# A hybrid decoder layer on one core: half of the per-layer projection moved into the local attention, and the last gate begun inside the MLP

## The chip, the cores and the metric

The kernel runs on one core of one Trainium2 chip. The metric is the device time of one execution in microseconds (us). Before the change the median of three runs is 864.67 us, the lowest 863.82 and the highest 864.80.

A core has five engines that matter here. TensorE (PE in the profile) multiplies matrices and turns (transposes) tiles, and its weight load is listed as PEld. VectorE (DVE) and ScalarE (ACT) do elementwise work. GpSimd (POOL) and SyncE (SP) mostly issue transfers (DMAs). [...]

## What is computed

The layer works on 512 tokens of width 1024. Its reference, cut to what matters here:

```python
h = rmsnorm(x, norm_mix_g)
proj = h @ w_in                                   # split into 9 parts
y_a = sigmoid(o_ml) * h_ml                        # mLSTM branch
y_b = swa_with_sinks(q_sw, k_sw, v_sw, sinks)     # local attention, 16 query heads, window 128
merged = sigmoid(g_a) * (y_a @ w_branch_a) + sigmoid(g_b) * (y_b @ w_branch_b)
x = x + merged @ w_out
x = x + square(relu(rmsnorm(x, norm_mlp_g) @ w_up)) @ w_down
gate = sigmoid(rmsnorm(x, norm_ple_g) @ w_ple_gate)
x = x + gate * (p @ w_ple_proj)                   # p: 512 x 256, w_ple_proj: 256 x 1024
out = rmsnorm(x, final_norm_g)
```

The per-layer projection is `p @ w_ple_proj`. It depends on inputs alone, so it can be done at any time before the gate is multiplied with it. In the text x2 is the value of x after the MLP, scaled by `norm_ple_g` and turned so that its 1024 features lie along the partitions: eight columns of 128 features, numbered 0 to 7. The gate product `x2 @ w_ple_gate` sums over these eight columns, two at a time, so that it has four chunks (numbers 0 to 3: columns 0 and 1, 2 and 3, 4 and 5, 6 and 7).

## The kernel before, in words

**Numbers.** Every float32 operand of a product is split into a high part and a low part (`split`, line 199): ACT casts the high part, DVE subtracts it from the value for the low part. A product is then three matmuls, high x high, high x low, low x high (`pairs`, line 233). A weight is loaded by SP into one of four raw buffers ("wr"), and its two parts go to one of four pairs of buffers ("wh", "wl") in `load_w` (line 221).

**Order.** The program is straight-line code for a list scheduler, which orders each engine's work ahead of time: what the code names first goes first as soon as its inputs are taken to be ready, and what comes later fills in. `tc.issue_after(i)` queues a block's instructions behind instruction `i` on `i`'s engine. `tc.keep_in_program_order` pins an instruction behind the one before it. For the MLP the class `Plan` (line 36) replaces this: its tasks have an engine, a cost and predecessors, the TensorE tasks stand in a written order, the others get due times from it, and `plan.run` emits all of them pinned (line 91).

**Stages.** First come the norm of x and the first half of the per-layer projection (512 of 1024 columns, `early_products`), whose result is parked in device memory in the tensor `ped` (lines 306 and 525). Then follow the input projections, the local attention (lines 865 to 968), the mLSTM, the branch products, the output projection, and the MLP in four quarters (`up_set`, `down`). The tail is what comes after `plan.run()` (line 1759).

**Local attention.** There are 16 units of scores and softmax (`swa_probs`, line 869), each with eight matmuls into a two-bank tile "psa", an eviction by DVE or ACT, and a softmax on both. Between the units the loop at line 961 pops a list `fill` of ten projections (line 957), one at each `u` that is not a multiple of three. A projection is 24 matmuls of 512 columns into one bank "psg"; there are two such banks (`ps_g`, line 157). `qk_proj` (line 849) empties its bank with one ACT instruction (line 852) and three DVE instructions (line 854).

**End of the MLP.** `down(3)` multiplies in seven products by sums and differences of blocks. The last of them (`w4`, line 1734) is two halves of 12 matmuls each into the two "psg" banks. Its result is added into `xk`, the running x, by `acc(Y, 0, 0)` (line 1735, DVE line 1690): tokens 0 to 255, feature columns 0 to 511. The columns 512 to 1023 are complete earlier, after line 1733.

**Tail.** `ple_rows` and `load_w(w_pp[1])` bring p and the second half of `w_ple_proj` and split them. `two_columns_of` (line 1208) turns two columns of x2 with eight transposes (line 1213) and splits them with `gple`, which is an ACT eviction (line 205) and a DVE one (line 206) for each column. Between them stand the four products `ple(m)` of six matmuls, which make the second half of the per-layer projection and are copied by ACT into `pe[m]` (line 1781). Then come the gate's first 512 output columns in four chunks of 24 matmuls (lines 1853 to 1861) into four banks `pv`, and then its second 512 columns with sigmoid, merge and final norm.

## Time and profile before

The profiled execution took 864.57 us by the clock of the runs; the span from its first to its last instruction is 862.7 us, so that 1.9 us lie around the span.

| what | value |
| --- | --- |
| median of the runs shown | 864.67 us |
| profiled execution | 864.57 us, span 862.7 us |
| granted TensorE clock | 0.998 |
| local attention, from first scores to the first branch product | about 228 to 322 us of the span |
| last half product of the MLP ends, tail begins | 801.4 us |
| second half of the gate begins | 832.4 us |
| last matmul ends | 855.3 us |

In the profile's groups each row names line, engine and operation, the output and input tiles, the shape, how often it ran, the busy time and the mean of one in ns, and the idle time before it. Matmuls overlap in the pipeline: a row gives each 0.39 us, but their starts are 0.227 us apart, and it is the distance of the starts that fills PE's time. In the timeline a row gives the start, the length, and in brackets the idle time before it with what ended it.

### The profile page before, as it was taken

What the parts mean: (1) busy time and instruction counts of PE and PEld (TensorE: products, weight loads), DVE (VectorE), ACT (ScalarE), POOL (GpSimd) and SP (SyncE); (2) the same over time, 40 slices, a digit from 0 to 9 for tenths busy, and PEclk for the clock granted to TensorE, in tenths of its full rate; (3) what the DMA queues carried; (4) which work ended last, traced back from release to release, by engine and by line L of the source; (5) the groups of instructions that cost most, each with busy time, mean ns of one, the idle gap of its engine ahead of it and who ended that gap; (6) DMA issues with size and microseconds to landing.
All of it is one profiled execution on the core that took longest, in us unless ns stands there. A gap on an engine that the chain in (4) does not pass through costs nothing.

```text
span 862.7 us, 12945 instructions
## 1 busy us (share of the span) xinstructions
PE 851.6 (99%) x4926; PEld 741.1 (86%) x4926; DVE 724.1 (84%) x1059; ACT 530.4 (61%) x913; POOL 61.2 (7%) x93
## 2 busy tenths in 40 slices
PE   9999999999999999999999999999999999999996
PEld 7888789999878777888888888899889989988886
DVE  7898879777788888867897799879988997899656
ACT  6776657555587667864343586458638744774743
POOL 3121111000000000000020000000000000010000
PEclk9999999999999999999999999999999999999999
DMA  8677235444411246565324381744365364634402
GB/s 289 204 179 295 89 144 189 155 147 146 148 49 50 98 147 226 202 252 200 122 39 133 98 234 38 221 129 137 75 193 147 104 174 133 172 104 131 138 1 97
DMA packets 37967, 125.70 MB, mean 146 GB/s; under 512 B 5261, under 2 KB 5261, under 8 KB 37906
## 3 DMA queue, kind: packets, MB, share of 16 engines
q1 hardware_dynamic: 28578, 95.77, 32.6%
q0 software_dynamic: 9184, 28.85, 13.9%
q8 instruction: 38, 0.62, 0.3%
q10 hardware_dynamic: 144, 0.26, 0.1%
q14 instruction: 23, 0.19, 0.1%
HBM read 106.51 MB, written 11.54 MB: 137 GB/s over the span
## 4 chain that ended last, share of the span: by engine, by line
PE 86%; issue 5%; DVE 4%; ACT 2%; DMA 2%; SPq 0%; POOL 0%; POOLq 0%; DVEq 0%; ACTq 0%
PE psp L1382 27%; PE psg L241 24%; PE psa L241 11%; PE psg L1382 9%; PE psp L241 6%; PE pst L241 4%; ACT lm L900 1%; DMA wr<-in_w_vsif 1%; PE psp L1213 1%; PE pst L945 1%; PE psa L875 1%; PE psa L876 1%; PE psa L911 1%; DVE wl L203 0%; DMA wh<-in_w_b 0%
## 5 line engine op out<-in xcount | busy, mean ns | idle before, releaser
L202 ACT CAST wh<-wr 128x1024 fp32r<-128x1024 f32 x90 | 94.8, 1054 | 81.1 <-PE psg L241 20.9
L203 DVE TENSOR_TENSOR wl<-wr,wh 128x1024 fp32r<-128x1024 f32 x90 | 109.5, 1220 | 35.7 <-ACT wh L202 35.3
L1382 PE MATMUL psp<-x,wh 128*128 128x256 f32 x672 | 121.3, 283 | 0.0
L1382 PE MATMUL psp<-wh,uf 128*128 128x512 f32 x336 | 106.1, 390 | 0.1
L1382 PEld LDWEIGHTS psp<-x,wh 128*128 128x128 f32 x672 | 105.0, 192 | 0.3
L1367 ACT CAST wh<-wr 128x1024 fp32r<-128x1024 f32 x59 | 60.5, 1049 | 59.7 <-DVE wr L1707 26.4
L1382 PE MATMUL psp<-x,wl 128*128 128x256 f32 x336 | 95.1, 283 | 0.0
L1370 DVE TENSOR_TENSOR wl<-wr,wh 128x1024 fp32r<-128x1024 f32 x59 | 71.2, 1219 | 10.3 <-ACT wh L1367 8.0
L1382 PEld LDWEIGHTS psp<-wh,uf 128*128 128x128 f32 x336 | 63.1, 188 | 14.3 <-issue 1.3
L1367 ACT CAST wh<-wd 128x1024 fp32r<-128x1024 f32 x45 | 47.2, 1049 | 33.0 <-PE psp L1382 27.8
L1382 PE MATMUL psp<-wl,uf 128*128 128x512 f32 x168 | 65.5, 390 | 0.0
L1382 PEld LDWEIGHTS psp<-x,wl 128*128 128x128 f32 x336 | 64.5, 192 | 0.0
L241 PE MATMUL psg<-h,wh 128*128 128x512 f32 x192 | 60.9, 395 | 0.7 <-DVE acc L854 0.7
L1370 DVE TENSOR_TENSOR wl<-wd,wh 128x1024 fp32r<-128x1024 f32 x45 | 54.7, 1218 | 3.1 <-ACT wh L1367 3.1
L241 PEld LDWEIGHTS psg<-h,wh 128*128 128x128 f32 x192 | 35.1, 188 | 7.5 <-DVE acc L854 0.9
L1400 DVE TENSOR_TENSOR uf<-F,uf 128x512 fp32r<-128x512 f32 (+3 forms) x36 | 35.0, 983 | 6.4 <-ACT uf L1399 6.4
L241 PE MATMUL psg<-yb,wh 128*128 128x512 f32 x128 | 40.0, 392 | 0.0
L241 PE MATMUL psg<-h,wl 128*128 128x512 f32 x96 | 37.7, 393 | 0.0
L1382 PEld LDWEIGHTS psp<-wl,uf 128*128 128x128 f32 x168 | 31.5, 188 | 6.7 <-DVE wl L1370 0.3
L1382 PE MATMUL psg<-wh,uf 128*128 128x512 f32 x112 | 36.5, 389 | 0.0
L1399 ACT CAST uf<-F 128x512 fp32r<-128x512 f32 (+3 forms) x36 | 30.7, 857 | 7.6 <-DVE F L1417 7.1
L241 PE MATMUL psg<-ya,wh 128*128 128x512 f32 x112 | 34.9, 391 | 0.0
(409 smaller groups left out, 2221.6 us busy)
## 6 DMA issues: line engine op xcount, KB each, us to landing
wr<-in_w_down SPq DMA_DIRECT2D x16, 512.0 KB, 4.6
wd<-in_w_down SPq DMA_DIRECT2D x16, 512.0 KB, 4.4
wr<-in_w_upb SPq DMA_DIRECT2D x12, 512.0 KB, 4.2
wd<-in_w_upb SPq DMA_DIRECT2D x12, 512.0 KB, 4.5
gd<-gr POOLq DMA_DIRECT2D x8, 512.0 KB, 2.9
wr<-in_w_qkml SPq DMA_DIRECT2D x8, 512.0 KB, 3.4
wr<-in_w_b SPq DMA_DIRECT2D x8, 512.0 KB, 3.4
wh<-in_w_b POOLq DMA_DIRECT2D x8, 512.0 KB, 4.6
```

What stands on the lines that cost most here:

```text
L202: A.copy(dst[0], src)
L203: last_low[0] = V.tensor_sub(dst[1], src, r32(dst[0]))
L241: last_mm[0] = T.matmul(ps, l, r, start=first and i == 0, stop=last and i == len(ops) - 1, skip_group_check=parts)
L875: T.matmul(o, q[:, n * P : (n + 1) * P], kk[kp][ab][:, k0 : k0 + 256], start=True, stop=False)
L876: T.matmul(o, q[:, n * P : (n + 1) * P], kl[kp][ab][:, k0 : k0 + 256], start=False, stop=True)
L900: A.activation(lm3[:, g, :], lm3[:, g, :], AF.Exp, bias=nmx[:, g : g + 1], scale=0.125, accum_out=sm[:, g : g + 1])
L911: T.transpose(pt[:, c : c + P], pT[:, c : c + P], ident)
L1367: return [A.copy(parts[0], slots[user])]
L1370: return [V.tensor_sub(parts[1], slots[user], r32(parts[0]))]
L1382: yield T.matmul(ps, l, r, start=first and j == 0, stop=last and j == len(ops) - 1, skip_group_check=True)
L1399: h = sca(n / 512 * 0.48 + 0.05, lambda: A.copy(dst()[0], src()), deps)
L1400: return vec(n / 512 * 0.54 + 0.06, lambda: V.tensor_sub(dst()[1], src(), r32(dst()[0])), [h])
```

## The change

Three things are done together. The second half of the per-layer projection becomes `ple_rest`, an eleventh entry of `fill`, and is stored to `ped`, which gets 1024 columns; the loop pops one entry more, at `u` = 0. The columns 4 to 7 of x2 are turned by `right_columns`, tasks of the plan that stand between the two halves of the last product. Chunk 2 of the gate becomes tasks of the plan too (`first_gates`), behind the last product. After the plan the columns 0 and 1 are turned, then chunk 3 follows, the columns 2 and 3, and the chunks 0 and 1. Each of these later chunks has its weight's cast queued on ACT behind the eviction of the columns turned last.

```diff
-    ped = dp.tile([P, NT, 512], F32, name="ped")
+    ped = dp.tile([P, NT, D], F32, name="ped")
...
-            nc.gpsimd.dma_start(out=ped[:, m, :], in_=early_pe[m])
+            nc.gpsimd.dma_start(out=ped[:, m, :512], in_=early_pe[m])
...
+    def ple_rest():
+
+        rows, w = load_w(p, 1024, 2), load_w(w_pp[1], 1024, 2)
+        for m in range(NT):
+            ps = ps_g()
+            mm_tok(ps, w, [[q[:, k, :] for q in rows] for k in range(2)], m)
+            t = act_f("pl")
+            A.copy(t, ps)
+            nc.gpsimd.dma_start(out=ped[:, m, 512:], in_=t)
...
-    fill = [lambda: qk_proj(0)] + [lambda i=i: q_proj(i) for i in range(5, 8)]
+    fill = [lambda: qk_proj(0), ple_rest] + [lambda i=i: q_proj(i) for i in range(5, 8)]
...
-        if u % 3:
+        if u % 3 or u < 3:
             fill.pop(0)()
...
-        acc(Z, 1, 1, u3)
-        w4, u4 = both(Y, A22, "b21", t4, False, True, y2)
+        z2 = acc(Z, 1, 1, u3)
+        w4[0], _ = half(Y, A22, "b21", 0, t4[0], False, True, y2)
+        if q == 3:
+            right_columns(sum(y2 + z2, []))
+        w4[1], u4 = half(Y, A22, "b21", 1, t4[1], False, True, y2)
         acc(Y, 0, 0, u4)
...
+    def turn(bank, k, m):
+        return T.transpose(bank[:, m * P : (m + 1) * P], xk[m][:, k * P : (k + 1) * P], ident)
+
+    def right_columns(deps):
...
+        spent = role[:2]
+        bank = lambda k: spent[k // 2 - 2][:, k % 2, :]
+        free = done_with[id(spent[0])] + done_with[id(spent[1])]
+        for k in range(4, KT):
+            v = plan.add("PE", 0.45, lambda k=k: (turn(bank(k), k, m) for m in range(NT)), deps + free + plan.last("PE"))
...
+            v = plan.add("ACT", 0.55, high, [v])
+            x2_ready[k] = vec(0.7, low, [v])
...
+    def first_gates():
+
+        X, Y, Z = role
+        w = form(("pg", 2), 2, [load("wr", w_pg[2], ("pg", 2))])
+        for m in range(NT):
+
+            def emit(got, m=m):
+                ops = []
+                for k in range(2):
+                    ops += pairs([q[:, m * P : (m + 1) * P] for q in x2[4 + k]], [q[:, k, :] for q in got])
+                return [(pv[m], ops, True, False)]
+
+            on_pe(w, 1.37, emit, [x2_ready[4], x2_ready[5]] + done_with[id(Z)])
...
+    pv = [role[0][:, 0, :], role[0][:, 1, :], role[2][:, 0, :], role[2][:, 1, :]]
+    first_gates()
     plan.run()
...
-    pT = ple_rows()
-
-    wp1 = load_w(w_pp[1], 2 * 512, 2)
...
+    def gate_chunk(c):
+        with tc.issue_after(turned_2[-1]) if turned_2 else ExitStack():
+            w = load_w(w_pg[c], 2 * 512, 2)
+        for m in range(NT):
+            ops = []
+            for k in range(2):
+                ops += pairs([q[:, m * P : (m + 1) * P] for q in x2[2 * c + k]], [q[:, k, :] for q in w])
+            chain(pv[m], ops, False, c == 1, True)
+
+    turned_2 = []
+
+    def left_columns(k, banks):
+        for c in range(2):
+            for m in range(NT):
+                turn(banks[c], k + c, m)
+        for c in range(2):
+            evicted = split(x2[k + c], banks[c], gple[:, k + c : k + c + 1])
+        turned_2.append(evicted.ins)
+        return evicted
+
+    left_columns(0, [role[1][:, 0, :], role[1][:, 1, :]])
+    gate_chunk(3)
+    evicted = left_columns(2, [ps_g(), ps_g()])
+    gate_chunk(0)
     nc.sync.dma_start(out=gfin, in_=g_fin.broadcast_to([P, D]))
     for m in range(NT):
-        nc.gpsimd.dma_start(out=pe[m][:, :512], in_=ped[:, m, :])
...
+        nc.gpsimd.dma_start(out=pe[m], in_=ped[:, m, :])
...
+    gate_chunk(1)
```

The old loops over `two_columns_of`, `ple` and the four chunks of `pv` go away. The second half of the gate and all that follows it are unchanged.

## Prediction

> **What bounds the kernel now.** I read the page first, then the chain of waits, then PE's waits, then the two places that the change touches, in windows and in the timeline.

> ```profile
> span 862.7 us, 12945 instructions
> PE 851.6 (99%) x4926; PEld 741.1 (86%) x4926; DVE 724.1 (84%) x1059; ACT 530.4 (61%) x913; POOL 61.2 (7%) x93
> PE 86%; issue 5%; DVE 4%; ACT 2%; DMA 2%; SPq 0%; POOL 0%; POOLq 0%; DVEq 0%; ACTq 0%
> ```

> PE is busy in 851.6 of 862.7 us, and the chain that ended last is PE for 86% of the span. The change takes no matmul and no transpose away; it moves them. So it can only gain what PE loses today, and it loses what PE will newly wait. PE's waits by name are few:

> ```profile
> PE psg L343 <- DVE zero L281: 1.1, 1, 1.1
> PE pst L945 <- DVE pT L918: 0.7, 1, 0.7
> PE psg L241 <- DVE acc L854: 0.7, 1, 0.7
> PE psa L875 <- DVE lm L889: 0.2, 1, 0.2
> PE psa L911 <- DVE nmx L893: 0.2, 1, 0.2
> ```

> The 1.1 us are the start and stay. Four waits lie in the local attention, 1.8 us in all, and the 0.7 of line 945 comes at its very end, after the last filler. What the new filler can cover at the beginning is 0.7 + 0.2 + 0.2 = 1.1 us. The windows say the same: outside 228 to 260 PE is full, and in the tail too.

> ```profile
> 228.00:246.00 18.00, 17.41 (x94) 14.26 (x93) 14.94 (x36) 14.34 (x44) 0.00 (x0) 1.00 0.17 60
> 246.00:260.00 14.00, 13.48 (x69) 9.49 (x70) 13.71 (x32) 10.54 (x37) 0.00 (x0) 1.00 0.27 79
> 260.00:275.00 15.00, 15.00 (x86) 12.84 (x86) 12.12 (x34) 11.07 (x40) 0.00 (x0) 1.00 0.20 67
> 801.40:810.80 9.40, 9.40 (x58) 7.93 (x57) 6.46 (x9) 7.19 (x12) 0.00 (x0) 1.00 0.16 63
> ```

> The columns are length, then busy time of PE, PEld, DVE, ACT and POOL, then PE's clock. PE lacks 0.59 and 0.52 us in the first two and nothing in the others. So the attention has about one microsecond to fill, and the change puts five into it.

> **Part 1, the projection in the attention.** It is 24 matmuls of 512 columns. The chain shows what such a group takes, and what sixteen transposes and the four gate chunks take:

> ```profile
> 265.58 5.45 PE psg L241 x24
> 484.35 1.75 PE psp L1213 x16
> 810.83 21.76 PE psp L241 x96
> ```

> The attention gets 5.44 us of PE work (21.76 / 4). On the other engines come two casts and four bank copies on ACT and two subtractions on DVE, by these rows of the tail, where their like stands today:

> ```profile
> 796.16 1.05 ACT L202 CAST wh<-wr 128x1024 fp32r<-128x1024 f32 x1 [1.66 <-PE psp L1382]
> 804.89 0.58 ACT L1781 COPY pe<-psg 128x512 f32<-128x512 f32 x1
> 808.67 1.22 DVE L203 TENSOR_TENSOR wl<-wr,wh 128x1024 fp32r<-128x1024 f32 x1 [0.51 <-ACT wh L202]
> 222.46 36.61 SPq L218 DMA_DIRECT2D wr<-in_w_qkml  x7
> ```

> ACT gets 2 x 1.05 + 4 x 0.58 = 4.4 us and DVE 2.4 us. From 228 to 260 ACT is free for 32 - 24.9 = 7.1 us and DVE for 32 - 28.65 = 3.35 us, and the stretch grows by five, so throughput suffices. On SP two loads now stand ahead of the later projections' weights; SP ran ahead there (seven loads spread over 36.6 us, waiting for raw buffers), so I take that at nothing; if a weight came late, PE would wait for its load. POOL gets four stores of 256 KB, and it was idle in these windows.

> What the filler needs is not engines but banks. A projection keeps one of the two "psg" banks until it is evicted, and this is how long that takes today:

> ```profile
> 236.49 0.39 PE L241 MATMUL psg<-h,wl 128*128 128x512 f32 x1
> 237.67 0.63 PE L241 MATMUL psg<-h,wh 128*128 128x512 f32 x2
> 242.91 0.39 PE L241 MATMUL psg<-h,wl 128*128 128x512 f32 x1
> 246.37 0.73 PE L241 MATMUL psg<-h,wh 128*128 128x512 f32 x2 [0.66 <-DVE acc L854]
> 236.98 0.40 ACT L900 ACTIVATE lm<-lm,nmx 128x128 f32<-128x128 f32 x1
> 241.90 0.67 ACT L852 ACTIVATE acc<-psg,cw 128x512 f32<-128x512 f32 x1
> ```

> The first projection's last matmul is at 236.49. ACT goes through the exponentials of three units from 236.98 to 241.90 and only then touches the bank, and DVE gives it back at 246.3, where PE has waited 0.66 us. In between PE lives on one projection of 5.4 us in the other bank (237.67 to 243.14). After the change the next filler is not one product of 24 matmuls in a bank but four of 6 (1.36 us each), and each wants its own eviction by ACT. If ACT keeps to its exponentials, the second bank is full at 237.67 + 1.36 = 239.0 and comes back at 241.90 + 0.58 = 242.5: 3.4 us in which PE has little else. They would replace the waits of 0.66 and 0.24 us seen there now, a net loss of 2.5 us. Against this, the first projection now precedes unit 2's scores in the code, and its eviction the softmax of unit 2, so the first bank should return earlier. The extra cost beyond 5.44 therefore lies between -1.1 (every wait filled) and +2.5. I take 0, nearer to the row of waits than to the row of the exponentials, because of that earlier place.

> **Part 2, the tail without the projection.** These rows bound it today:

> ```profile
> 801.41 0.38 PE L1213 MATMUL psp<-ident,xk 128*128 128x128 f32 x2
> 810.66 0.39 PE L241 MATMUL psp<-wh,x 128*128 128x512 f32 x1
> 832.42 0.39 PE L241 MATMUL psg<-wh,x 128*128 128x512 f32 x1
> ```

> From the first transpose to the first matmul of the gate's second half are 832.42 - 801.41 = 31.01 us. What must still be done there (or, for the right columns, inside the last product) is 32 transposes, 2 x 1.75 = 3.50, and the four chunks, 21.76: together 25.26. So 5.75 us go: 5.44 of the projection and 0.3 of switching. That holds if PE does not wait.

> **Part 3, the right columns.** They need the additions after the last but one product:

> ```profile
> 796.17 1.41 DVE L1690 SCALAR_TENSOR_TENSOR xk<-psp,r,xk 128x512 f32<-128x512 f32 x2 [0.41 <-PE psp L1382]
> 796.13 5.44 PE psg L1382 x24
> 801.61 0.75 DVE L1690 SCALAR_TENSOR_TENSOR xk<-psg,r,xk 128x512 f32<-128x512 f32 x1 [0.61 <-PE psg L1382]
> ```

> Those are done at 797.6; the first half of the last product ends at 796.13 + 2.72 = 798.85, so the transposes start without a wait. The second half (2.72 us) covers the eviction of columns 4 and 5, and chunk 2 finds them ready. These transposes are pinned, and behind them queue the rest of the last product and chunk 2: were the additions late by more than 1.2 us, all of that would shift. The last addition (801.61 to 802.36 today) is covered by chunk 2's 5.44 us.

> **Part 4, the new wait.** When chunk 2 ends (call it T), PE turns columns 0 and 1. Chunk 3 needs only the columns 6 and 7, which are ready, but its weight's cast is queued on ACT behind the eviction of column 1. Today the first chunk's weight is cast at 796.16, fourteen microseconds before its use at 810.66; that cover is gone. The new chain, by these rows and those above:

> ```profile
> 803.53 1.45 ACT L205 ACTIVATE x<-psp,gple 128x512 fp32r<-128x512 f32 x2 [6.31 <-PE psp L1213]
> 807.54 1.10 ACT L202 CAST wh<-wr 128x1024 fp32r<-128x1024 f32 x1
> L1213 PE MATMUL psp<-ident,xk 128*128 128x128 f32 x64 | 8.0, 273 | 0.0
> ```

> Column 0 is turned at T + 0.44 + 0.27 = T + 0.71. Two evictions, 1.45, end at T + 2.16. The cast, 1.10, ends at about T + 3.2 (ACT's rows overlap by 0.1), and chunk 3's first matmul can go. The second needs the low part, 1.22 on DVE: T + 4.4. PE's eight transposes end at T + 0.87; the transposes of columns 2 and 3 can fill to T + 1.74. Then PE stands for 1.46 us, does the first matmul of each of the four banks (0.91 us), and stands 0.3 us more: 1.8 us. The ends are 0 (the transposes slip in during chunk 2, so that the evictions are over at T) and 3.5 (nothing fills T + 0.87 to T + 4.4). I take 1.8, because today's list puts transposes of a later pair ahead wherever PE is free. The chunks 0 and 1 have 5.44 us of cover each.

> Of the transfers, the load of `pe` is twice as large and the final gain's load moves back in SP's queue:

> ```profile
> L1776 POOL DMA_DIRECT2D pe<-ped x4: 898/900/909, 767.7 to 769.4; - x4
> L1810 DVE TENSOR_TENSOR prod<-sgp,pe x11: 415/426/692, 830.6 to 855.9; 128x256 f32<-128x256 f32 x6, 128x512 f32<-128x512 f32 x5
> DMA to landing us min/median/max: 5.9/6.7/8.3
> ```

> The first use is at 830.6 and the loads are issued at 768; even at 16.6 us, twice the longest landing, they are hidden by some 45 us.

> **The sum.** Against the execution's own 864.57 us: -5.75 + 1.8 (tail) + 5.44 + 0 (attention) = +1.5, so 866.1 us. That execution is 0.1 us below the median of 864.67. About 0.2% (1.7 us: 862.9 to 866.4) is what a measurement of this kernel can tell from no change, so the forecast is no measurable change, on its slow side.

> **The rivals.**
> *The banks stall the attention (slower).* One mechanism: two banks, four small products and an ACT that is in the exponentials. It decides where ACT's copy of the first small product is put behind the third unit's exponentials. For it: ACT ran without a break from 236.98 to 241.90, and the bank of line 852 waited for it. Against it: the earlier place of the first projection. Price: +2.5, 868.6 us.
> *The tail does not wait.* If the left transposes find gaps in chunk 2, the 1.8 us vanish: 864.57 - 5.75 + 5.44 = 864.3, no change. For it: the list does move work forward. Against: chunk 2 is pinned, always ready, and named earlier.
> *Everything fills (faster).* The same, and the attention's 1.1 us are covered, and the 0.7 at its end too because the softmax has got ahead: 864.3 - 1.8 = 862.5. Against it: three conditions at once.
> *The clock falls.* The window behind the last matmul shows PE's clock after idleness:

> ```profile
> 855.00:857.00 2.00, 0.32 (x3) 0.11 (x1) 1.26 (x4) 1.63 (x2) 0.00 (x0) 1.00 0.68 262
> 858.00:859.00 1.00, 0.00 (x0) 0.00 (x0) 0.49 (x1) 0.46 (x1) 0.00 (x0) 1.00 0.00 0
> 859.00:860.00 1.00, 0.00 (x0) 0.00 (x0) 0.00 (x0) 0.00 (x0) 0.00 (x0) 0.53 0.65 252
> ```

> PE ends at 855.3, and the clock halves at about 859.1, 3.7 us later. Chunk 2's end is followed by 1.7 us of transposes and 1.5 us of waiting, 3.2 us without an ordinary matmul. If transposes counted as idleness and the pause grew a little, the next 3.7 us would run at half speed: +1.85, 867.9 us. [...] The row of 801.40 to 810.80 has 32 transposes with the clock at 1.00, but matmuls lie between them, so no run here shows it yet.

> **How the numbers follow.** Forecast 0.40 (its own range 865.3 to 866.9; 0.30 within 0.2%, 0.10 slower), banks 0.27 (slower), no wait in the tail 0.18 (0.15 within, 0.03 faster), everything fills 0.10 (faster), clock 0.05 (slower). Together faster 0.13, same 0.45, slower 0.42. The range reaches from 863.0, near the case in which everything fills, to 868.9, just over the bank case; outside are the rest of the fast case and the 3.5 us end of the tail's wait on top of the bank case.

> **What would show it.** In the profile after: the tail's stretch from the end of the last product to the first 256-column matmuls shorter by about 4 us; an idle time of PE of 1 to 2 us before chunk 3, ended by ACT line 202 or DVE line 203; the attention longer by about 5.4 us; its waits on DVE line 854 gone, or in their place a wait on the ACT copy of `ple_rest`. I am wrong if chunk 3 starts without a wait, if PE stands over 2 us between 236 and 248, or if any part before 228 or between 360 and 795 changes its length.

## The result, and the profile after

The changed kernel takes 874.92 us (median of five runs, 873.29 to 875.90), the kernel before 864.80 (863.82 to 864.98): a ratio of 1.0117, 95% interval 1.0102 to 1.0132. It is slower by 10 us, and the forecast of 866.1 us with its range to 868.9 was wrong. The profiled execution took 875.62 us. The head of its page:

```profile
span 873.8 us, 12968 instructions
PE 856.6 (98%) x4926; PEld 743.4 (85%) x4926; DVE 724.6 (83%) x1059; ACT 530.6 (61%) x913; POOL 63.5 (7%) x97
```

The span grew by 11.1 us, and PE's busy time by 5.0 although PE has the same 4926 instructions. So one part of the loss is standing, and another is that the same matmuls take longer. PE's waits (in total, how often, the longest; the 1.1 us of the start left out):

```profile
PE psg L241 <- ACT pl L872: 4.0, 1, 4.0
PE psp L241 <- ACT wh L202: 2.6, 1, 2.6
...
PE psa L1035 <- DVE hd L1059: 0.9, 1, 0.9
PE psg L241 <- DVE acc L854: 0.4, 2, 0.3
```

The first two are new. One lies in the attention, one in the tail.

**The attention.** ACT's timeline (start, length, instruction), then PE's:

```profile
235.46 1.05 ACT L202 CAST wh<-wr 128x1024 fp32r<-128x1024 f32 x1 [3.98 <-PE psg L241]
236.53 1.28 ACT L907 ACT_TABLE_LOAD   x1
237.83 0.20 ACT L907 ACTIVATE es<-ds 128x4 f32<-128x4 f32 x1
...
241.23 0.69 ACT L852 ACTIVATE acc<-psg,cw 128x512 f32<-128x512 f32 x1
...
242.29 0.60 ACT L872 COPY pl<-psg 128x512 f32<-128x512 f32 x1
```

```profile
238.66 0.28 PE L886 MATMUL psa<-kl,qs 128*128 128x256 f32 x1
242.94 0.50 PE L241 MATMUL psg<-wh,wh 128*128 128x512 f32 x1 [4.00 <-ACT pl L872]
...
243.92 0.63 PE L241 MATMUL psg<-wh,wh 128*128 128x512 f32 x1
244.35 0.63 PE L241 MATMUL psg<-wl,wh 128*128 128x512 f32 x1
```

PE finishes the projection's first product at 237.8 and a unit's scores at 238.9. Then both "psg" banks (128 x 512 float32 each, by these rows) are full, one with the convolution's product, one with this one. ACT is in the exponentials of two units from 237.83 to 241.21, does two other evictions, and copies the bank out from 242.29 to 242.89; PE's next product into it starts at 242.94. The product that waits is the second of the projection (its four start at 236.44, 242.94, 245.58 and 248.40); the expectations below call it the third. Afterwards the starts of the matmuls are 0.43 us apart, not 0.227: PE runs at half its clock (0.50 in the windows below).

**The tail.** First PE, then ACT:

```profile
809.68 1.91 PE L1759 MATMUL psp<-ident,xk 128*128 128x128 f32 x16
811.34 0.48 PE L1392 MATMUL psg<-wh,uf 128*128 128x512 f32 x1
...
819.62 1.03 PE L1759 MATMUL psp<-ident,xk 128*128 128x128 f32 x8
820.49 1.04 PE L1759 MATMUL psg<-ident,xk 128*128 128x128 f32 x8
824.10 0.80 PE L241 MATMUL psp<-wh,x 128*128 128x512 f32 x1 [2.57 <-ACT wh L202]
```

```profile
820.69 0.69 ACT L205 ACTIVATE x<-psp,gple 128x512 fp32r<-128x512 f32 x1 [7.51 <-PE psp L1759]
821.28 1.26 ACT L205 ACTIVATE x<-psg,gple 128x512 fp32r<-128x512 f32 x2
822.42 0.70 ACT L205 ACTIVATE x<-psp,gple 128x512 fp32r<-128x512 f32 x1
822.99 2.95 ACT L202 CAST wh<-wr 128x1024 fp32r<-128x1024 f32 x3
```

The right columns are turned and chunk 2 runs without a wait. Then ACT evicts column 0, the columns 2 and 3 (x2, out of "psg"), and only then column 1, and chunk 3's cast is queued behind that. PE stands for 2.57 us, and about 0.5 more for the low part (its wait is listed as 0.5 us, ended by DVE line 203, in the tail alone; here it lies within the half clock).

**The clock.** These windows are the cells of a grid of 3.41 us (how the grid was found stands at the end). The fields with a multiplication sign are busy time and instructions of PE, PEld, DVE, ACT and POOL; the number behind them is PE's clock:

```profile
240.10:243.51 3.41, 0.57 (x2) 0.48 (x3) 2.81 (x6) 3.25 (x10) 0.33 (x1) 1.00 0.07 28
243.51:246.92 3.41, 3.23 (x8) 2.13 (x7) 3.41 (x8) 1.29 (x8) 0.21 (x1) 0.50 0.19 77
...
820.37:823.78 3.41, 1.16 (x11) 0.92 (x9) 2.37 (x4) 3.09 (x5) 0.00 (x0) 1.00 0.01 2
823.78:827.19 3.41, 3.06 (x6) 2.01 (x7) 3.41 (x5) 3.41 (x6) 0.00 (x0) 0.50 0.25 66
827.19:830.61 3.42, 3.42 (x9) 2.67 (x8) 2.86 (x5) 3.35 (x8) 0.00 (x0) 0.50 0.89 291
```

A cell in which PE hardly worked (busy 0.57 and 1.16 us) is followed by one, or two, at half clock: 3.4 us in the attention, 6.8 us in the tail.

**The balance.** Before, the last product starts at 795.97 and the gate's second half at 832.42; after, at 806.95 and 843.82. So the tail takes 36.87 us instead of 36.45, and the other 11.0 us arise ahead of it. There: 5.4 of moved work, 4.0 of standing for the bank, 1.7 of half clock, 0.7 more ahead of line 1035, less 1.2 of old waits (the attention's 1.8 us of them shrank to 0.6): 10.6, which leaves about 0.4 without a name. In the tail: -5.75 + 2.6 + 0.5 + about 3 of half clock = +0.4.

The theory to be tested (called W): two stands, each behind a FIFO on ACT, and a clock that falls because PE stands.

### The profile page after: what moved, and what is told of

The parts are those of the page before. It is cut to its first block, busy times and chain, and to the rows that moved or that the text cites. A ratio compares the mean times of both kernels' runs of the same rounds, so it can differ in the third digit from the quotient of the medians.

```text
span 873.8 us, 12968 instructions
## 1 busy us (share of the span) xinstructions
PE 856.6 (98%) x4926; PEld 743.4 (85%) x4926; DVE 724.6 (83%) x1059; ACT 530.6 (61%) x913; POOL 63.5 (7%) x97
## 4 chain that ended last, share of the span: by engine, by line
PE 86%; issue 5%; DVE 5%; ACT 2%; DMA 0%; POOL 0%; POOLq 0%; DVEq 0%; ACTq 0%
PE psp L1392 28%; PE psg L241 24%; PE psa L241 11%; PE psg L1392 9%; PE psp L241 5%; PE pst L241 4%; PE pst L955 1%; ACT lm L910 1%; ACT wh L202 1%; DVE wl L203 1%; PE psa L885 0%; DMA wh<-in_w_b 0%; DVE acc L854 0%; PE psa L921 0%; PE psa L886 0%
## 5 line engine op out<-in xcount | busy, mean ns | idle before, releaser
L202 ACT CAST wh<-wr 128x1024 fp32r<-128x1024 f32 x90 | 94.2, 1052 | 86.9 <-PE psg L241 27.6
L203 DVE TENSOR_TENSOR wl<-wr,wh 128x1024 fp32r<-128x1024 f32 x90 | 109.5, 1221 | 38.5 <-ACT wh L202 38.0
L1380 DVE TENSOR_TENSOR wl<-wr,wh 128x1024 fp32r<-128x1024 f32 x60 | 72.4, 1219 | 11.5 <-ACT wh L1377 9.3
L241 PE MATMUL psg<-h,wh 128*128 128x512 f32 x192 | 60.6, 394 | 0.3 <-DVE acc L854 0.3
L241 PEld LDWEIGHTS psg<-h,wh 128*128 128x128 f32 x192 | 35.4, 188 | 8.2 <-issue 0.8
L241 PE MATMUL psg<-yb,wh 128*128 128x512 f32 x128 | 40.2, 393 | 0.0
L241 PE MATMUL psg<-h,wl 128*128 128x512 f32 x96 | 37.9, 395 | 0.0
L241 PE MATMUL psg<-ya,wh 128*128 128x512 f32 x112 | 34.9, 391 | 0.0
```

Of the source, the lines that this page charges most:

```text
L202: A.copy(dst[0], src)
L203: last_low[0] = V.tensor_sub(dst[1], src, r32(dst[0]))
L241: last_mm[0] = T.matmul(ps, l, r, start=first and i == 0, stop=last and i == len(ops) - 1, skip_group_check=parts)
L1380: return [V.tensor_sub(parts[1], slots[user], r32(parts[0]))]
```

## The experiments

Each kernel was timed beside the kernel before on the same chip; the kernel before had medians of 864.27 (beside each part alone, chunk 3's cast first, and the copies on DVE), 864.04 (beside the three casts, the spare banks, the later place and the added matmuls) and 864.45 (beside the last four). Beside the changed kernel it had 864.80, so a gain over the changed kernel, given below as a difference of medians, is up to 0.8 us smaller when each kernel is set against the kernel before beside it.

### One part at a time

The attention part alone: the kernel before, plus (the function `ple_rest` and the wider `ped` left out here)

```diff
-    fill = [lambda: qk_proj(0)] + [lambda i=i: q_proj(i) for i in range(5, 8)]
+    fill = [lambda: qk_proj(0), ple_rest] + [lambda i=i: q_proj(i) for i in range(5, 8)]
...
-        if u % 3:
+        if u % 3 or u < 3:
...
```

> The kernel before, with the new projection function in the list of fillers and the tail untouched, so that the second half of the per-layer projection is computed twice (the tail uses its own). It holds the attention part of the change and nothing else. Theory W (waits and clock): the added 24 matmuls cost 5.4 us, the third product stands 4.0 us on its bank because the copy that empties it is queued on ACT behind two units' exponentials, and the clock is halved for some 3 us behind that, 1.4 us: with the small waits that shift, about +11 us, so near 876. The forecast's own bounds: +4.3 to +7.9, so 869 to 873. Rival S (the loss belongs to the sum of both parts, for instance a memory layout that the new tail brings): +5.4, so 870, and no stand of over 1 us ahead of the projection's third product.

Measured: 876.62 us, ratio 1.0146 (1.0129 to 1.0164). PE's waits:

```profile
PE psg L241 <- ACT pl L872: 4.0, 1, 4.0
PE psa L1035 <- DVE hd L1059: 2.2, 1, 2.2
```

The tail alone, which is the changed kernel without `ple_rest`:

```diff
-    fill = [lambda: qk_proj(0), ple_rest] + [lambda i=i: q_proj(i) for i in range(5, 8)]
+    fill = [lambda: qk_proj(0)] + [lambda i=i: q_proj(i) for i in range(5, 8)]
...
+            nc.gpsimd.dma_start(out=ped[:, m, 512:], in_=early_pe[m])
...
```

> The changed kernel without the new projection function: the second half of the per-layer projection is left out, and the first half's values stand in its place. It holds the tail part of the change and nothing else. Theory W: from the last product's start to the second half of the gate the tail takes what it took before or 0.4 us more, since the 5.75 us that go are eaten by a wait of 2.6 us ahead of the third chunk and 3 us of half clock behind it: 865, no difference that can be measured. The forecast: 5.75 us go and 1.8 come back, so 861. Rival S: the wait ahead of the third chunk comes from what the attention part moved, and is gone here: 859.

Measured: 863.40 us, ratio 0.9988 (0.9979 to 0.9997). The wait is there without the attention part:

```profile
PE psp L241 <- ACT wh L202: 2.6, 1, 2.6
```

The whole loss is in the attention part, 12.4 us; the tail part gains 0.9 us of its 5.75. Their sum, 11.5, is within 1.5 us of the change's 10.1, so rival S falls. The stand of 4.0 us is the same to the tenth.

### The tail's wait

```diff
-    left_columns(0, [role[1][:, 0, :], role[1][:, 1, :]])
-    gate_chunk(3)
+    w3 = load_w(w_pg[3], 2 * 512, 2)
+    left_columns(0, [role[1][:, 0, :], role[1][:, 1, :]])
+    gate_chunk(3, w3)
...
```

> The changed kernel, with the load and cast of the weights of the tail's chunk 3 issued ahead of the left columns, so that the cast isn't queued on ACT behind any of their evictions. Theory W: the wait of 2.6 us goes, the clock then has no reason to fall (3.2 us), and 0.3 us of waiting for the low parts goes: -6, so 869. Rival K (chunk 3 waits for something that comes just after the cast, or the cast only moves the wait to the next chunk): -1 or less, so 874. Rival C (the clock falls because of the 16 transposes and not because of the wait): -2.6, so 872, and the granted clock still falls to 0.5 in the tail.

Measured: 875.27 us (872.64 to 878.50), ratio 1.0131 (1.0108 to 1.0154): no gain at the median. ACT's timeline and PE's wait show that the wait has moved:

```profile
826.85 1.26 ACT L205 ACTIVATE x<-psg,gple 128x512 fp32r<-128x512 f32 x2 [3.72 <-PE psg L1759]
828.00 1.99 ACT L202 CAST wh<-wr 128x1024 fp32r<-128x1024 f32 x2
```

```profile
PE psp L241 <- ACT wh L202: 1.9, 1, 1.9
```

Chunk 3 went without a wait, and chunk 0 stood instead, for its own cast behind the evictions of columns 2 and 3. That is rival K; theory W, which took the wait for gone, was too quick. The profiled execution is one of the shortest. It has no half clock in the tail, which takes 33.71 us in it, 3.2 less than in the changed kernel. The two longest had the lowest mean clocks (0.990 and 0.991, the others 0.993 to 0.995); what else they lost was not recorded. The next kernel takes all three casts out of the queue:

```diff
+    w3, w0, w1 = [load_w(w_pg[c], 2 * 512, 2) for c in (3, 0, 1)]
     left_columns(0, [role[1][:, 0, :], role[1][:, 1, :]])
-    gate_chunk(3)
+    gate_chunk(3, w3)
...
```

> The changed kernel, with the loads and casts of the weights of all three later chunks of the tail (3, 0 and 1) issued ahead of the left columns. ACT stood idle for 5 to 6 us between the right columns' evictions and the left ones', and three casts take 3.2 us. Where chunk 3's cast alone went first, PE stood 1.9 us for chunk 0's cast instead, behind the evictions of columns 2 and 3. Theory W (each chunk's cast is queued on ACT behind evictions; stands of PE cost their own length and, where they leave a grid cell of 3.41 us with less than about 1.4 us of PE work, 1.7 or 3.4 us more in half clock): no stand over 0.5 us from the last product to the second half of the gate, and no half clock there: -2.9 of waits and -1.7 to -3.4 of clock, 869 to 870. Rival K (the left columns or the low parts come last, and the wait moves once more, to chunk 0's columns or DVE's low parts): 872 to 875, with a stand ended by DVE L206 or L203.

Measured: 869.52 us, ratio 1.0064 (1.0051 to 1.0076), 5.4 us under the changed kernel. One window from the last product to the second half of the gate:

```profile
806.00:843.50 37.50, 37.50 (x184) 31.42 (x183) 23.26 (x34) 23.04 (x37) 0.00 (x0) 1.00 0.21 71
```

PE has no gap and the full clock. (The list now also puts the transposes of the columns 2 and 3 behind the start of chunk 3.) From the last product's start to the gate's second half it takes 30.79 us; 36.45 - 5.75 = 30.70 had been worked out for a tail without waits.

### The bank in the attention

```diff
-            A.copy(t, ps)
+            V.tensor_copy(t, ps)
```

> The changed kernel, with the four copies that empty the projection's banks put on DVE instead of ACT. DVE stood idle from 237.8 to 239.6 us in the profile after, just when the first copy was wanted. Theory W: the stand of 4.0 us ahead of the third product falls under 1 us and the clock stays up behind it; the copies take 4 x 0.7 us on DVE and cost up to 1 us where they delay the convolution: -4.5, so 870 (869 to 872). Rival L (load: the added work of ACT and DVE is what slows the attention, whichever engine has it, as the units behind it wait for their probabilities): no gain, 874 to 876, with the wait moved to the score or turn instructions.

Measured: 874.84 us, ratio 1.0124 (1.0110 to 1.0138). The stand shrinks only from 4.0 to 2.4 us. From the first full scores (near 228) to the first branch product the profiled execution takes 105.1 us, against 105.9 in the changed kernel and 94.9 before, and the median doesn't move. DVE's timeline:

```profile
239.13 0.16 DVE L911 TENSOR_TENSOR sm<-sm,es 128x4 f32<-128x4 f32 x1 [1.84 <-ACT lm L910]
...
239.54 0.69 DVE L914 TENSOR_TENSOR lm<-lm,rc 128x512 f32<-128x512 f32 x1
240.15 0.68 DVE L872 COPY pl<-psg 128x512 f32<-128x512 f32 x1
```

DVE was idle for 1.84 us, but with line 911 at the head of its queue, which waited for ACT's exponentials, and the copy stood behind it and began at 240.15. The idle time was no help to an instruction that was queued behind a waiting one. A cell at half clock was left as well (the clock is 0.83 from 237 to 243 and 0.76 from 243 to 246). This run alone would have spoken for rival L. Other banks tell the two apart:

```diff
-            ps = ps_g()
+            ps = ps_g() if m == 2 else ps_t()
```

> The changed kernel, with the projection's products 0, 1 and 3 written to the pair of one-bank tiles that the attention's sums use only later, and product 2 to the pair shared with the weight projections. The copies stay on ACT where they were. Theory W: three products run without a stand, the fourth waits for the first's copy (near 243) for about 1.2 us; no half clock: -2.8 of waits and -1.7 to -3.4 of clock, 870 to 871. Rival L (ACT and DVE are what the attention waits for, and PE only waits somewhere else if it doesn't wait here): the stand moves to the next weight projection or to a turn (ended by DVE L854 or L894) and the time stays at 874 to 875.

Measured: 869.12 us, ratio 1.0061 (1.0048 to 1.0074), 5.8 us under the changed kernel:

```profile
PE psp L241 <- ACT wh L202: 2.6, 1, 2.6
PE psa L1035 <- DVE hd L1059: 1.6, 1, 1.6
PE pst L241 <- ACT pl L872: 1.3, 1, 1.3
```

ACT and DVE have as many instructions as before (913 and 1059), and on ACT the same exponentials and evictions still stand ahead of the first copy; what follows it the list has put in another order. The 4.0 us are 1.3, no half clock follows in the attention, and its stretch takes 100.8 us instead of 105.9. So it was the banks, and rival L falls. The same function three places later in the list:

```diff
-    fill = [lambda: qk_proj(0), ple_rest] + [lambda i=i: q_proj(i) for i in range(5, 8)]
+    fill = [lambda: qk_proj(0)] + [lambda i=i: q_proj(i) for i in range(5, 8)] + [ple_rest]
```

> The changed kernel, with the projection put fifth in the list of fillers (behind the query projections 5 to 7) and not second. Its banks, its copies on ACT and its length are the same. Theory W (its stand comes from the one burst of ACT work at the pipeline's start: a table load and the exponentials of two units, back to back, while all units' scores that the banks allow are done): no stand over 1 us and no half clock in the attention; -4.0 and -1.7 to -3.4: 868 to 870. Rival Q (four evictions in 5.4 us on two banks are too many anywhere in this stage, where ACT always has a unit's exponentials queued): stands of 2 to 4 us show up at the new place, 872 to 876.

Measured: 872.79 us, ratio 1.0098 (1.0084 to 1.0112), 2.1 us better, about a third of what theory W said, and within rival Q's range. The projection itself no longer waits, and none of Q's stands of 2 to 4 us appears. But the scores and turns wait, in pieces of up to 0.9 us:

```profile
PE psa L885 <- DVE lm L899: 1.4, 2, 0.7
...
PE psa L921 <- DVE lm L894: 0.9, 1, 0.9
PE psg L241 <- DVE acc L854: 0.7, 1, 0.7
```

Two of them lie within one cell of the grid (266.57 to 269.98, 1.80 us in the busy column), and a cell at half clock (0.50) follows. Neither theory had this, and why the pieces arise there was not tested.

### The clock

Twelve matmuls more in each of the two stands (the code also names chunk 3 behind the transposes of the columns 2 and 3, where PE did it anyway):

```diff
             mm_tok(ps, w, [[q[:, k, :] for q in rows] for k in range(2)], m)
+            if m == 0:
+                spare_bank = ps_t()
+                for _ in range(12):
+                    T.matmul(spare_bank, rows[0][:, 0, :P], w[0][:, 0, :], start=True, stop=True)
...
+    for i in range(12):
+        T.matmul(pv[i % NT], zero, x2[4][0], start=False, stop=False, skip_group_check=True)
...
```

> The changed kernel with added matmuls in its two stands, and nothing else in another place: twelve products of the projection's operands into a bank that nobody reads, behind the projection's first product, and twelve products with a matrix of zeros, accumulated into the gate's banks, behind the left columns' transposes. The results stay as they are, and so do the waits: the third product still has to wait for ACT's copy (until about 243) and chunk 3 for its cast. 12 x 0.227 = 2.7 us of the stands of 4.0 and 2.6 us are filled. Theory W: the clock is what falls when PE stands, so no half clock in the attention or in the tail; the time falls by what the half clock cost, 1.7 to 3.4 us in each place in a run: -3 to -5, 870 to 872. Rival N (the half clock belongs to the place, for instance to the burst of ACT work or to power, and not to PE's stand): no change or up to 0.5 us more, 875.

Measured: 870.83 us, ratio 1.0074 (1.0061 to 1.0088): PE does 5.4 us of useless work more, and the kernel is 4.1 us faster. The cells of both places:

```profile
239.96:243.37 3.41, 2.14 (x14) 1.75 (x13) 2.81 (x7) 2.92 (x9) 0.55 (x1) 1.00 0.01 4
243.37:246.78 3.41, 3.41 (x19) 2.77 (x18) 3.34 (x9) 2.21 (x10) 0.55 (x1) 1.00 0.37 153
...
823.63:827.04 3.41, 3.41 (x16) 2.80 (x15) 3.41 (x6) 3.38 (x7) 0.00 (x0) 1.00 0.73 229
```

```profile
242.47 0.50 PE L241 MATMUL psg<-wh,wh 128*128 128x512 f32 x1 [1.27 <-ACT pl L876]
```

Line 876 is the copy in this kernel. The projection's second product still begins when ACT's copy is done, 6.50 us behind the start of the first, as in the changed kernel; and chunk 3 still begins 4.5 us behind the end of chunk 2. So the ends of the waits have not moved. What went is the half clock. Rival N falls. With transposes in the attention's stand, and the tail as changed:

```diff
+                for i in range(24):
+                    T.transpose(spare_bank[:, i % NT * P : (i % NT + 1) * P], ident, ident)
```

> The changed kernel, with 24 transposes of the identity into a bank that nobody reads, behind the projection's first product; the tail is the changed kernel's. 24 x 0.109 = 2.6 us of the attention's stand of 4.0 us are filled with transposes and not with ordinary matmuls. Theory G (any PE work counts for the clock; the next cell of the 3.41 us grid is at half clock where PE worked under about 1.36 us in this one): no half clock between 238 and 252, so -1.7 to -3.4: 872 to 873. Rival P (transposes don't count as PE work for the clock, as my forecast's fifth case took it): half clock for one or two cells from about 242, as in the changed kernel, 875.

Measured: 871.16 us, ratio 1.0078 (1.0064 to 1.0092). No half clock in the attention:

```profile
240.19:243.60 3.41, 2.04 (x17) 1.79 (x16) 2.77 (x7) 3.38 (x12) 0.14 (x1) 1.00 0.11 46
243.60:247.01 3.41, 3.41 (x18) 2.79 (x17) 3.41 (x8) 1.73 (x8) 0.95 (x2) 1.00 0.22 89
817.05:820.46 3.41, 1.61 (x15) 1.37 (x13) 1.92 (x3) 2.64 (x5) 0.00 (x0) 1.00 0.00 0
820.46:823.87 3.41, 2.12 (x8) 1.46 (x9) 3.41 (x5) 3.41 (x4) 0.00 (x0) 1.00 0.14 26
```

The clock stayed at 1.00 behind the 24 transposes, and rival P falls; the clearest case is the cell at 817.05, which would hold 0.03 us of work without its transposes (counted by the starts) and is followed by the full clock. The last two rows hold this profile's own tail, with the same wait of 2.6 us. Here the grid cuts the wait in two, PE is busy for 1.61 and 2.12 us in its two cells, and no half clock follows. In the kernel with the spare banks most of it lies in one cell, where PE is busy for 1.14 us, and the next is at half clock:

```profile
818.43:821.84 3.41, 1.14 (x4) 0.67 (x5) 3.41 (x5) 3.41 (x5) 0.00 (x0) 1.00 0.01 2
821.84:825.25 3.41, 3.41 (x10) 2.63 (x9) 3.41 (x6) 3.39 (x7) 0.00 (x0) 0.50 0.72 240
```

### Both cures, and what is left

The spare banks and the three early casts together:

> The changed kernel with both cures: the projection's products 0, 1 and 3 in the sums' banks, and the casts of chunks 3, 0 and 1 ahead of the left columns. Theory W: the two gains add up, since they lie in different stages: 874.9 - 5.8 - 5.4 = 863.7 (863 to 865), no difference from the kernel before that can be measured, because 1.3 us of the projection's wait for a bank and 1 to 2 us of the wait for DVE's copies of the matrix memory's stage (about 365 us) are left. Rival A (what one cure gives, the other takes back, for instance the clock's grid or the loads that start earlier): 866 to 869.

Measured: 864.41 us, ratio 1.0003 (0.9991 to 1.0014). The gains add up to within 1 us, and with both cures the change neither gains nor loses measurably. PE's waits that the projection brought are down to

```profile
PE pst L241 <- ACT pl L872: 1.3, 1, 1.3
PE psa L1035 <- DVE hd L1059: 1.1, 2, 0.7
```

The second one, at line 1035 (the matrix memory), stands at 0.2 us in the kernel before (line 1025 there), and at 0.2 to 2.3 us in the kernels with the projection in the attention. PE waits there for a copy of two columns on DVE. In the changed kernel DVE starts that copy at 367.15, behind a subtraction (line 228) that begins at 366.01, when a weight transfer of POOL has just landed, at 365.99. To take it away too, on top of both cures:

```diff
-            A.copy(t, ps)
+            (A.copy if m else V.tensor_copy)(t, ps)
...
-            V.tensor_copy(hd[:, h, 2 * half : 2 * half + 2], pn[:, :, DV])
+            A.copy(hd[:, h, 2 * half : 2 * half + 2], pn[:, :, DV])
```

> The kernel with both cures, and two things more: the copy of the projection's first product on DVE (so that its bank is free near 240.2 and the fourth product doesn't wait), and the two small copies of the matrix memory's normalizers (DVE's instruction at 1059 that PE waits for near 365) on ACT, where DVE's wait for a weight transfer doesn't hold them up. Theory W: the 1.3 us of the bank and the 1 to 2 us near 365 go as well: 861 to 862, faster than the kernel before by 2 to 3 us. Rival D (PE has no work ahead at these places, and the stands come back a little later): 863.5 to 864.5.

And its second edit alone in the kernel before:

> The kernel before, with the two small copies of the matrix memory's normalizers on ACT instead of DVE, and nothing else. In its profile PE stands 0.2 us for them near 357. Theory W (the wait of 0.9 to 2.3 us at this place in the kernels with the projection in the attention is a consequence of the change, as the margin that PE had there is gone): 864, no difference that can be measured. Rival H (the kernel before pays for the same wait in most of its runs, and its profile shows a lucky one): 862.5 to 863.

Measured: 864.06 us (0.9996, 0.9987 to 1.0004) and 863.87 us (0.9990, 0.9982 to 0.9999). In the first, both waits are gone but for 0.4 us, and a new one of 1.3 us has come behind a unit's scores near 270:

```profile
PE psg L241 <- DVE qs L554: 1.3, 1, 1.3
```

That fits rival D: what PE doesn't wait for here it waits for a little later. In the second, 0.1% is at the edge of what can be told. No version with the projection in the attention beats the kernel before by a measurable amount. Why the margin at line 1035 shrinks when the projection lies in the attention was not found.

## Why the prediction was wrong

**The move itself was worked out rightly.** Forecast were 5.44 us more in the attention and 5.75 less in the tail. With both cures the stretch from the scores to the branch products is 5.9 us longer (5.44, and 1.3 of bank wait that is left, less about 0.9 of old waits); the tail is 5.65 shorter. The rival "the tail does not wait", 864.3, is near what that kernel measured, 864.4, in part by luck: it had neither that bank wait nor the 1.1 us at line 1035, nor the old waits that went. The claims that the engines' throughput suffices and that the right columns are turned without a wait (part 3) held as well.

**Part 1, the bank: the failed step.** The price of the stall was put between -1.1 and +2.5, and 0 was taken "nearer to the row of waits than to the row of the exponentials", because the first projection's earlier place should return its bank earlier. It did, at 245.53 instead of 246.3, but that was the wrong bank to look at. PE stood for the second one, and the chain for that was written down: full at 239.0, back at 242.5. In the profile it is full at 237.8, PE has no other work from 238.9 on, and the bank is back at 242.9. So the rival's mechanism was right, and the earlier place was no argument against it: ACT's copy stood behind the exponentials, of two units where the rival said three. It cost 4.0 us, less 1.2 of old waits: 2.8, against 2.5. That was outside the price's own bounds of -1.1 to +2.5, and the half clock behind it came on top.

**Part 4, the wait before chunk 3: right mechanism, small size.** 1.8 us were taken, out of 0 to 3.5; it was 2.6 + 0.5 = 3.1. The step that was off is "Two evictions, 1.45, end at T + 2.16". With T = 819.62, the first eviction began at T + 1.07, after all eight transposes and not after four (T + 0.71), and the list put the evictions of columns 2 and 3 between those of columns 0 and 1. So the cast ended at 824.05, T + 4.4, and not T + 3.2. The prediction used the early transposes of 2 and 3 as PE's cover and forgot that each turned column also brings an eviction to ACT's queue.

**The clock: right in kind, wrong in cause and place, and mis-sized.** It had a chance of 0.05, only in the tail, and only if transposes counted as idleness. No run shows that they did: behind the 24 transposes in the attention the cell from 243.60 had the full clock (1.00). The stands alone did it, in both places. It cost about 1.7 + 3 us in the profiled execution, and 4.1 us came back at the median when added matmuls kept the clock up (3.3 when each kernel is set against the kernel before beside it). In the prediction's own rows the clock fell 3.7 us after the last matmul, and it was concluded that a pause must be about that long. In the changed kernel's tail it fell at 823.78, 2.25 us after PE's last transpose had ended (821.53), so a pause need not be that long.

**The range: cases taken one at a time.** The banks, the tail's wait and the clock were priced as alternatives. They sit in different places and can all happen, and two of them cause the third. The profile's sum is 1.5 (forecast) + 2.8 (bank) + 1.3 (more wait in the tail) + 4.7 (clock) + 0.7 (line 1035, which the prediction did not have) = 11.0; between the two profiled executions lie 875.62 - 864.57 = 11.05 us.

## What to carry to other kernels

Price a product by the banks that it fills, not only by its matmuls: four products of 1.4 us want four evictions where one of 5.4 us wants one, and each eviction stood in a FIFO behind whatever ACT or DVE had been given before (here ACT's copy began at 242.29, 4.5 us after its bank was full), even while that waited (1.84 us on DVE). Where an instruction is queued behind an eviction, count every eviction that the list may put ahead of it. And a stand of PE can have a second price, the half clock behind it (3.41 us of it behind the stand of 4.0 us, 6.83 behind the one of 2.6 in the changed kernel, and a cell of 3.41 behind one of 2.2 in the attention part alone); rivals of different stages are to be added before the range is drawn.

## What the runs showed of the hardware

Whether half clock followed a cell went with PE's work in it. I counted it by the starts (0.227, 0.121 and 0.109 us for each product, score and transpose), since the busy column above uses modelled ends and comes out higher. In the changed kernel's profile the cells ahead of the half clock hold 0.45 us (from 240.10) and 0.98 us (from 820.37), and no other at full clock, ahead of the cell in which the last matmul falls, holds less than 1.88; in the profile before none holds less than 2.3, and the clock stays at 1.00 until PE has ended. Over all these profiles, ahead of the cell in which the last matmul falls, the eleven full-clock cells with up to 1.29 us were followed by half clock, and those with 1.30 us or more were not. (The first 9 to 13 us of each profile are left out: there the windows show a clock of 1.00 where none is recorded, and the starts, 0.43 us apart, are those of half clock.) The cells of 1.29 and 1.30 us are closer than such a count can tell apart, so it gives no exact border. A cell at half clock with up to 1.36 us of work, counted in the same way, was followed by another (from 823.78 in the changed kernel, 1.36 us), one with 1.59 or more by the full clock (from 243.51 and 827.19 there, 1.59 and 1.82 us). So the same wait of 2.6 us cost no clock in one profile (the transposes in the attention) and 1.7 us in another (the spare banks, 3.41 us at 0.50), by where the grid fell. A stand of 2.2 us was enough in the attention part alone: PE is busy for 1.22 us in the cell from 366.45, and the next one is at 0.50. This kernel's float32 transposes kept the clock up as its products did: the cell filled by them (1.45 us by the starts, with hardly anything else, at 817.05, above) was followed by the full clock.
